# First copies of the down weights' sums: from GpSimd's DMA queue to fixed slots of SP's weight queue

## The chip, the cores and the metric

One core of a Trainium2 chip. The metric is the device time of one execution in microseconds (us), lower is better; the median of several runs is given, and one execution was taken with the hardware profiler. Engines: PE (TensorE, matmuls; PEld its weight loads), ACT (ScalarE), DVE (VectorE), POOL (GpSimd), SP (SyncE, which here only issues DMAs). 16 DMA engines serve all queues of the core; the DMAs that SP issues run on queue q1 and those that POOL issues on q0.

## The reference, cut to what matters

Two decoder layers on 256 tokens of width 2048 in float32: block attention in the first, sliding-window attention with 4 key/value heads in the second, each followed by a convolved, gated feed-forward network with a hidden width of 5504, and a layer norm behind each part:

```python
def conv_ffn(x, w_up, conv_w, conv_b, w_down):
    h = x @ w_up                      # 2048 -> 2 * 5504
    hc = causal_depthwise_conv(h, width 3) + conv_b
    g, v = jnp.split(hc, 2, axis=-1)
    return (jax.nn.gelu(g) * v) @ w_down   # 5504 -> 2048
```

All weights are used once, so each passes through on-chip memory once per run: 770 half-megabyte pieces and a bit.

## The kernel before, in words

**Precision.** Each float32 operand is split into a high part (rounded to the PE's fast format) and a low part, and a product is computed as high x high, high x low and low x high. For weights ACT makes the high part (`high_upto`, L124) and DVE the low part by subtraction (`low_piece`, L133).

**The weight stream.** Weights come from DRAM in "halves" of 128 x 1024 floats (512 KB). A list `source` fixes their order for the whole run. `load_weights` (L98 to L108) issues the next half's DMA on SP (L105) into one of four `raw` buffers; `split_upto` splits a half and then issues the load that takes over its raw buffer; four pairs of buffers hold split halves, besides spare homes in tiles that are idle around a stage's end. `take()` hands the next half to the matmuls and first splits up to three halves ahead. So SP, which executes its instructions in program order, waits in each load until a raw buffer is free, and is paced by PE.

**Slots.** One half's matmuls make a `step()`, which counts the slot up. `at(n, f)` puts a piece of work into the program n slots on; it is written there, in program order, on whichever engine executes it. An engine that waits for none of the stage's data is free to execute it much earlier than PE reaches that slot.

**Up phase.** `FeedForward.run` computes the up-projection in 86 units of two halves (172 slots per layer). The first four units are the "opening" (`ws_opening`, L310 and L322): it uses the first 128 tokens' half of the normalized input first, so that it may start while the second is still being normalized. The other units are `ws_unit`: 8 matmuls with high weights (L292), 8 with low ones (L295) per half. ACT and DVE do the convolution, gate and split of the hidden values beside that.

**Sums for the down phase.** The down-projection computes some products in groups ("quads"), where pairs of hidden blocks and pairs of output column chunks are multiplied with sums of weights and sums of activations, which takes fewer matmuls. There are 16 quads in layer 0 and 18 in layer 1. The sums of weights are formed in DRAM by the DMA engines alone, in a tensor `t` of two halves per quad, by `sum_weights` (L249): steps 0 and 1 copy two blocks into each of t[0] and t[1] (L260, plain copies of 512 KB from DRAM to DRAM); step 2 adds a third block to both parts of t[0] (L262, 512 KB); step 3 adds t[0]'s first part to both parts of t[1] (L264, 512 KB); step 4 adds the fourth block to one part of t[1] (L266, 256 KB). The adding steps are accumulating DMAs issued by POOL; in this kernel the copies are issued by POOL too. `plan_sums` (L268) places the five steps of quad j at slots n0 + j * step + (0, 2, 5, step + 1, step + 4) of the up phase, with n0 = 2 and step = (4 * 43 - 20) // (quads + 3), which is 8 in layer 0 and 7 in layer 1. The down phase loads the sums through the weight stream like any other half (`raw<-t`).

**Around the up phase.** Ahead of it lies the attention's output projection (`project_out`, L345 to L347) with the layer norm: `evac` and `moments` (L438, L443, L565) gather the statistics on DVE, `norm` (L576, L577) applies them, `turn` (L586) transposes on PE. In its last column chunk `late` and `reach` split halves further ahead than usual, into spare homes, so that the opening's eight halves are there. The feed-forward stage's first DMA on POOL is the load of the convolution's weights (L829); in layer 0 four copies of the second layer's bias bands (L276) follow it, and then the sums.

Of the kernel before, what the change touches and what calls it, by code (L numbers as in the profile page):

```python
# [25 lines left out]
FT = DFF // P  # L26
# [23 lines left out]
QUADS = ((10, 6), (10, 8))  # L50
# [23 lines left out]
def trunk(ctx: ExitStack, tc: tile.TileContext, wst, wq, xT_in, x_in, relb, onehot, umask, sinks, conv_in, ln_g, ln_b, out):  # L74
    nc = tc.nc
# [59 lines left out]
    def split_upto(i, behind=None):  # L135
        while todo["low"] <= min(i, n_halves - 1):
            s = todo["low"]
            high_upto(s, behind)
            if len(pieces(s)) == 1:
                low_piece(s, slice(0, HW))  # L140
            placed.pop(s)
            raws.pop(s)
            load_weights()
            todo["low"] += 1
# [4 lines left out]
    def at(n, f, *a, first=False):  # L149

        fs = before.setdefault(slot["now"] + n, [])
        fs.insert(0 if first else len(fs), (f, a))
# [5 lines left out]
    def run(agenda):  # L158
        for n in sorted(n for n in agenda if n <= slot["now"]):
            for f, a in agenda.pop(n):  # L160
                f(*a)  # L161

    def step():
        run(behind)
        slot["now"] += 1
# [3 lines left out]
    def take(ahead=AHEAD):  # L169
        i = nexth["i"]  # L170
        nexth["i"] += 1
        if i in reach:
            run(before)
        split_upto(max(i + ahead, reach.get(i, 0)))
        run(before)
        return halves.pop(i)
# [72 lines left out]
    def sum_weights(q, i):  # L249


        j, t = QUAD_LIST.index(q), tsum[q]
        block = lambda a, b: wq[j][:, a:a + b, :]
        half = lambda k: t[k].rearrange("p (a b) -> p a b", b=512)

        def twice(a):
            return bass.AP(tensor=a.tensor, offset=a.offset, ap=[a.ap[0], [0, 2], [1, 512]])

        if i < 2:
            nc.gpsimd.dma_start(half(i), block(i, 2))  # L260
        if i == 2:
            nc.gpsimd.dma_start(half(0), twice(block(3, 1)), accum_op=ALU.add)  # L262
        if i == 3:
            nc.gpsimd.dma_start(half(1), twice(t[0][:, 0:512]), accum_op=ALU.add)  # L264
        if i == 4:
            nc.gpsimd.dma_start(t[1][:, 512:], wq[j][:, 1, :], accum_op=ALU.add)  # L266

    def plan_sums(l, n0, step):  # L268

        for j, q in enumerate(q for q in QUAD_LIST if q[0] == l):  # L270
            for i, m in enumerate((0, 2, 5, step + 1, step + 4)):
                at(n0 + j * step + m, sum_weights, q, i)
# [25 lines left out]
    def ws_opening(accs, between, done):  # L298

        n0 = nexth["i"]
        nexth["i"] += 2 * len(accs)
        run(before)
        pair = [[halves.pop(n0 + 2 * u + i) for i in range(2)] for u in range(len(accs))]

        def high(u, t, ks):
            part = lambda a: a.rearrange("p (s t c) -> p s t c", s=2, t=2)[:, :, t, :]
            for k in ks:
                nc.tensor.matmul(part(accs[u]), cols(pair[u][k // 8][0], k % 8), part(xT[:, k, :]),  # L310
                                 start=(t == 0 and k == 0), stop=False)

        for u in range(len(accs)):
            between(u)
            high(u, 0, range(KB))
        for c in range(KB // 4):
            between(len(accs) + c)
            for u in range(len(accs)):
                high(u, 1, range(4 * c, 4 * c + 4))
        for u, acc in enumerate(accs):  # L320
            for k in range(KB):
                nc.tensor.matmul(acc[:, 0:T], cols(pair[u][k // 8][1], k % 8), xT[:, k, 0:T],  # L322
                                 start=False, stop=(k == KB - 1))
            step()
            step()
            done(u)
            run(before)

    class Moving:
# [5 lines left out]
        def block(self, ahead=AHEAD):  # L335
            if self.pos % 2 == 0:
                self.half = take(ahead)
            j = self.pos % 2
            self.pos += 1
            return [w[:, j * 512:(j + 1) * 512] for w in self.half]  # L340
# [42 lines left out]
    def acc_tile():  # L383
        return psum.tile([P, 512], F32, name="acc")
# [4 lines left out]
    def four_sums(f0, f1, out):  # L389

        x = ((f0[:, 0:P], f1[:, 0:P]), (f0[:, P:T], f1[:, P:T]))
        s = lambda i: out[:, (i - 1) * P:i * P]
        minus(s(1), x[1][0], x[1][1])
        minus(s(2), s(1), x[0][0])
        minus(s(3), x[0][0], x[1][0])
        nc.vector.tensor_tensor(out=s(4), in0=x[0][1], in1=s(2), op=ALU.add)
# [419 lines left out]
    class FeedForward:  # L816
# [29 lines left out]
        def run(self, rest):  # L846
            l, pool = self.l, self.pool
            norm, (turn, low) = rest
            n0 = nexth["i"]
            cc = COLS[1]  # L850
            for c in cc[:3]:
                norm(c)

            def between(i):
                if i == OPENING - 1:
                    low(cc[0], turn(cc[0]))
                    norm(cc[3])
                if OPENING <= i < OPENING + 3:
                    c = cc[i - OPENING + 1]
                    low(c, turn(c))  # L860
                    if i > OPENING:
                        split_upto(n0 + i + 1)

            def conv(i, s, acc, c):
                w = self.cw[:, i, s, :]
                h = self.place(0)
                nc.scalar.activation(h, acc[:, T:2 * T], AF.Copy)  # L867
                nc.vector.tensor_tensor(out=h, in0=acc[:, 0:T], in1=h, op=ALU.add)  # L868
                nc.vector.tensor_scalar(c, h, w[:, 2:3], w[:, 3:4], op0=ALU.mult, op1=ALU.add)  # L869
                nc.vector.scalar_tensor_tensor(c[:, 1:T], h[:, 0:T - 1], w[:, 1:2], c[:, 1:T], op0=ALU.mult, op1=ALU.add)  # L870
                nc.vector.scalar_tensor_tensor(c[:, 2:T], h[:, 0:T - 2], w[:, 0:1], c[:, 2:T], op0=ALU.mult, op1=ALU.add)  # L871

            def gate(i, g, v):
                nc.vector.tensor_tensor(out=g, in0=g, in1=v, op=ALU.mult)

            def store(i, g):
                b = self.block(i)
                nc.scalar.activation(b[:, 0:T], g, AF.Copy)
                nc.vector.tensor_tensor(out=b[:, T:2 * T], in0=g, in1=b[:, 0:T].bitcast(F32), op=ALU.subtract)

            cs, gs, early = {}, {}, []

            def sums(p):
                if not early:
                    early.append(gbp.tile([P, 2 * D], F32, name="gb"))
                four_sums(gs.pop(2 * p), gs.pop(2 * p + 1), early[0][:, p * 512:(p + 1) * 512])

            def after(u, acc):
                i, s = divmod(u, 2)
                cs[s] = self.place(1 + s)  # L890
                at(0, conv, i, s, acc, cs[s])
                if s == 0:
                    at(1, nc.scalar.activation, cs[0], cs[0], AF.Gelu_apprx_tanh)
                else:
                    at(0, gate, i, cs[0], cs[1])
                    at(1, store, i, cs[0])
                    if i < 2 * S_EARLY:
                        gs[i] = cs[0]
                        if i % 2:
                            at(1, sums, i // 2)  # L900

            plan_sums(l, 2, (4 * FT - 20) // (sum(QUADS[l]) + 3))
            accs = [acc_tile() for _ in range(OPENING)]

            def opened(u):
                after(u, accs[u])
                if u < 2:
                    split_upto(n0 + 2 * OPENING + 2 * u + 1)

            ws_opening(accs, between, opened)  # L910
            for u in range(OPENING, 2 * FT):
                acc = acc_tile()
                ws_unit(acc)
                after(u, acc)
            homes = None
            if l == 0:
                x, h = ([(tile, j) for j in range(n)] for tile, n in ((xT, SPARE), (st, 4)))
                homes = lambda: (x + HALF_BUFS * [None], h + [(self.up, j) for j in range(2)])
            return project_out(self.block, FT, 2 * l + 1, homes, AF.Exp,
                               paired=self.work.rearrange("p a b -> p (a b)"), early_sums=early[0])  # L920
# [123 lines left out]
```

## Time and profile before

| | |
|---|---|
| median of 3 runs | 2104.02 us (2103.35 to 2106.24) |
| profiled execution | 2101.43 us, span of its instructions 2099.7 us |
| PE busy | 98% of the span |
| DVE, ACT, POOL busy | 74%, 50%, 7% |
| bytes moved by DMA | 512.07 MB, of them 416.71 on q1 and 93.24 on q0 |
| mean granted clock of PE | 0.991 |

How to read it: "busy" counts an engine's instructions without its waits; DMA-issuing instructions are not busy time on SP. In the row of 40 slices each digit is the busy share of 52.5 us in tenths. A row of the busy time by stretches has, behind the stretch, its length, then PE, PEld, DVE, ACT and POOL busy with the number of instructions, the granted PE clock, the mean busy share of the 16 DMA engines, and GB/s. The chain of waits is followed back from the last instruction: start, length, what it was waiting for or executing. A row of a queue in the DMA view gives packets, MB, and the time of its packets as a share of 16 engines over the stretch; a row of issues gives the tensors, count, size, and the median time from issue to landing. In a row of the order of time the bracket is the idle time before the instruction and what ended it.

### The profile page before, as it was taken

What the parts mean: (1) busy time and instruction counts of PE and PEld (TensorE: products, weight loads), DVE (VectorE), ACT (ScalarE), POOL (GpSimd) and SP (SyncE); (2) the same over time, 40 slices, a digit from 0 to 9 for tenths busy, and PEclk for the clock granted to TensorE, in tenths of its full rate; (3) what the DMA queues carried; (4) which work ended last, traced back from release to release, by engine and by line L of the source; (5) the groups of instructions that cost most, each with busy time, mean ns of one, the idle gap of its engine ahead of it and who ended that gap; (6) DMA issues with size and microseconds to landing.
All of it is one profiled execution on the core that took longest, in us unless ns stands there. A gap on an engine that the chain in (4) does not pass through costs nothing.

```text
span 2099.7 us, 29222 instructions
## 1 busy us (share of the span) xinstructions
PE 2058.1 (98%) x10974; PEld 1776.7 (85%) x10974; DVE 1547.2 (74%) x2292; ACT 1049.0 (50%) x1467; POOL 151.4 (7%) x196
## 2 busy tenths in 40 slices
PE   9999999799999999999999999889999999999997
PEld 8888888698888888888888888778888888888886
DVE  5655555688888787787776676578888788787767
ACT  5444443345544555465563554435454454455553
POOL 0000001212111000000000000111111100000000
PEclk9999999899999999999999999989999999999999
DMA  8665549999999555578885546989999965558884
GB/s 317 208 221 199 175 167 307 239 280 299 299 296 286 191 189 183 191 264 305 287 284 206 172 145 201 314 223 284 300 303 283 293 212 188 189 203 289 301 295 165
DMA packets 156718, 512.07 MB, mean 244 GB/s; under 512 B 17648, under 2 KB 22320, under 8 KB 155296
## 3 DMA queue, kind: packets, MB, share of 16 engines
q1 hardware_dynamic: 119072, 416.71, 56.3%
q0 software_dynamic: 37216, 93.24, 20.0%
q8 instruction: 86, 1.41, 0.3%
q14 instruction: 56, 0.46, 0.1%
q10 hardware_dynamic: 288, 0.26, 0.0%
HBM read 507.97 MB, written 86.56 MB: 283 GB/s over the span
## 4 chain that ended last, share of the span: by engine, by line
PE 89%; DMA 7%; DVE 2%; ACT 1%; issue 0%; ACTq 0%; POOL 0%; DVEq 0%; POOLq 0%
PE acc L292 38%; PE acc L295 20%; DMA raw<-in_wst_dram 6%; PE acc L546 4%; PE acc L545 4%; PE acc L547 4%; PE acc L345 3%; PE acc L347 3%; PE acc L346 3%; PE acc L310 1%; PE at L546 1%; PE at L547 1%; PE at L545 1%; DMA raw<-t 1%; DVE wl L133 1%; PE acc L322 1%
## 5 line engine op out<-in xcount | busy, mean ns | idle before, releaser
L133 DVE TENSOR_TENSOR wl<-raw,wh 128x1024 fp32r<-128x1024 f32 (+1 forms) x716 | 870.7, 1218 | 447.0 <-ACT wh L124 438.6
L124 ACT ACTIVATE wh<-raw 128x1024 fp32r<-128x1024 f32 (+1 forms) x716 | 755.4, 1056 | 709.1 <-DMA raw<-in_wst_dram 218.3
L292 PE MATMUL acc<-xT,wh 128*128 128x512 f32 x3456 | 872.7, 394 | 0.0
L292 PEld LDWEIGHTS acc<-xT,wh 128*128 128x128 f32 x3456 | 623.4, 189 | 112.9
L295 PEld LDWEIGHTS acc<-xT,wl 128*128 128x128 f32 x3456 | 471.4, 190 | 33.9
L295 PE MATMUL acc<-xT,wl 128*128 128x256 f32 x3456 | 481.8, 282 | 0.0
L545 PE MATMUL acc<-wh,up 128*128 128x512 f32 x336 | 130.8, 389 | 0.0
L546 PE MATMUL acc<-wl,up 128*128 128x512 f32 x336 | 130.8, 389 | 0.0
L547 PE MATMUL acc<-wh,up 128*128 128x512 f32 x336 | 130.7, 389 | 0.0
L870 DVE SCALAR_TENSOR_TENSOR work<-work,cw 128x255 f32<-128x255 f32 x172 | 83.2, 484 | 6.1
L871 DVE SCALAR_TENSOR_TENSOR work<-work,cw 128x254 f32<-128x254 f32 x172 | 83.1, 483 | 6.2
L260 POOL DMA_DIRECT2D t<-in_wq_dram x68 | 76.1, 1119 | 0.0
L869 DVE TENSOR_SCALAR work<-work,cw 128x256 f32<-128x256 f32 x172 | 71.1, 413 | 6.2
L547 PEld LDWEIGHTS acc<-wh,up 128*128 128x128 f32 x336 | 63.1, 188 | 13.2
L545 PEld LDWEIGHTS acc<-wh,up 128*128 128x128 f32 x336 | 63.1, 188 | 13.1
L546 PEld LDWEIGHTS acc<-wl,up 128*128 128x128 f32 x336 | 63.1, 188 | 13.0
L868 DVE TENSOR_TENSOR work<-acc,work 128x256 f32<-128x256 f32 x172 | 71.7, 417 | 1.5 <-ACT work L867 1.5
L161 ACT ACTIVATE work<-work 128x256 f32<-128x256 f32 x86 | 35.9, 418 | 61.6 <-DVE work L871 61.5
L867 ACT ACTIVATE work<-acc 128x256 f32<-128x256 f32 x172 | 62.7, 365 | 6.5 <-PE acc L322 6.5
L264 POOL DMA_DIRECT2D t<-t x34 | 35.6, 1046 | 345.1 <-issue 174.7
L133 DVE TENSOR_TENSOR up<-raw,up 128x1024 fp32r<-128x1024 f32 x30 | 36.5, 1221 | 29.6 <-ACT up L124 29.5
L345 PE MATMUL acc<-wh,xT 128*128 128x512 f32 x144 | 57.8, 401 | 0.0
(209 smaller groups left out, 2227.4 us busy)
## 6 DMA issues: line engine op xcount, KB each, us to landing
raw<-in_wst_dram SPq DMA_DIRECT2D x704, 512.0 KB, 4.6
t<-in_wq_dram POOLq DMA_DIRECT2D x102, 512.0 KB, 11.7
raw<-t SPq DMA_DIRECT2D x68, 512.0 KB, 4.5
t<-t POOLq DMA_DIRECT2D x34, 512.0 KB, 8.3
t<-in_wq_dram POOLq DMA_DIRECT2D x34, 256.0 KB, 7.3
gb<-in_ln_g_dram POOLq DMA_DIRECT2D x4, 1024.0 KB, 8.6
gb<-in_ln_b_dram POOLq DMA_DIRECT2D x4, 1024.0 KB, 11.7
band<-ud SPq DMA_DIRECT2D x4, 512.0 KB
```

The costliest lines, as they stand in the source:

```text
L124: nc.scalar.activation(wh[:, c], raws[s][:, c], AF.Copy)
L133: nc.vector.tensor_tensor(out=wl[:, c], in0=raws[s][:, c], in1=wh[:, c].bitcast(F32), op=ALU.subtract)
L260: nc.gpsimd.dma_start(half(i), block(i, 2))
L292: nc.tensor.matmul(acc, cols(wh, j), xT[:, k, :], start=(k == 0), stop=False)
L295: nc.tensor.matmul(o, cols(wl, j), xT[:, k, 0:T], start=False, stop=(k == KB - 1))
L345: nc.tensor.matmul(acc, sh, wh, start=(k == 0), stop=False)
L545: nc.tensor.matmul(bank(key), a[0], wh[:, c], start=key not in begun, stop=False)
L546: nc.tensor.matmul(bank(key), a[0], wl[:, c], start=False, stop=False)
L547: nc.tensor.matmul(bank(key), a[1], wh[:, c], start=False, stop=stop)
L868: nc.vector.tensor_tensor(out=h, in0=acc[:, 0:T], in1=h, op=ALU.add)
L870: nc.vector.scalar_tensor_tensor(c[:, 1:T], h[:, 0:T - 1], w[:, 1:2], c[:, 1:T], op0=ALU.mult, op1=ALU.add)
L871: nc.vector.scalar_tensor_tensor(c[:, 2:T], h[:, 0:T - 2], w[:, 0:1], c[:, 2:T], op0=ALU.mult, op1=ALU.add)
```

## The change

Steps 0 and 1 of each quad's sum, the plain copies into `t`, are issued by SP instead of POOL, at their slots of the up phase, so in SP's program order they stand between weight loads. The accumulating steps stay on POOL; the first of them now waits for copies that were issued on another engine. The plan begins at slot 12 instead of 2, and the distance between quads becomes (4 * 43 - 30) // (quads + 3): 7 slots instead of 8 in layer 0, 6 instead of 7 in layer 1. Neither copy carries a wait in SP's program. All other lines are as before; line numbers behind `plan_sums` are higher by one.

```diff
@@ sum_weights
         if i < 2:
-            nc.gpsimd.dma_start(half(i), block(i, 2))
+            nc.sync.dma_start(half(i), block(i, 2))
         if i == 2:
             nc.gpsimd.dma_start(half(0), twice(block(3, 1)), accum_op=ALU.add)
@@ plan_sums
         for j, q in enumerate(q for q in QUAD_LIST if q[0] == l):
             for i, m in enumerate((0, 2, 5, step + 1, step + 4)):
                 at(n0 + j * step + m, sum_weights, q, i)
@@ FeedForward.run
-            plan_sums(l, 2, (4 * FT - 20) // (sum(QUADS[l]) + 3))
+            plan_sums(l, 12, (4 * FT - 30) // (sum(QUADS[l]) + 3))
```

## The prediction

> **What bounds the kernel now.** I read the page first, the engines' shares and the 40 slices; then busy time by stretches, the chain of waits, POOL's order of time, and the DMA view of single stretches.
>
> ```profile
> PE 2058.1 (98%) x10974; PEld 1776.7 (85%) x10974; DVE 1547.2 (74%) x2292; ACT 1049.0 (50%) x1467; POOL 151.4 (7%) x196
> ```
>
> ```profile
> POOL 0000001212111000000000000111111100000000
> ...
> DMA  8665549999999555578885546989999965558884
> ```
>
> PE is busy 98%, so at most 41.6 us (2099.7 less 2058.1) can be won from its idle time. POOL works in two stretches, slices 6 to 12 and 25 to 31, one per layer, and there the DMA row stands at 9: POOL does nothing else there than issue the sums' transfers. So the sums are not spread over the up phase; they run as one burst. The busy time by stretches puts the idle PE at the head of each burst:
>
> ```profile
> 360.00:380.00 20.00, 18.90 (x82) 14.89 (x82) 9.62 (x8) 7.81 (x8) 4.00 (x5) 1.00 1.03 320
> 380.00:400.00 20.00, 6.04 (x23) 4.75 (x22) 14.92 (x20) 7.25 (x9) 3.69 (x5) 0.63 0.99 284
> ```
>
> ```profile
> 1340.00:1360.00 20.00, 18.72 (x82) 14.82 (x81) 8.55 (x7) 7.20 (x7) 4.10 (x6) 1.00 1.02 297
> 1360.00:1380.00 20.00, 8.05 (x30) 6.32 (x29) 15.88 (x22) 7.38 (x10) 1.58 (x2) 0.66 0.94 267
> ```
>
> The second number is PE busy of 20 us: idle 1.10 + 13.96 = 15.1 us in layer 0, 1.28 + 11.95 = 13.2 us in layer 1; the DMA share (last but one) is about 1. This is the end of the attention projection, with the layer norm and the opening of the up phase behind it. The chain of waits there:
>
> ```profile
> 318.17 8.78 DMA raw<-in_wst_dram
> ...
> 381.95 8.78 DMA raw<-in_wst_dram
> ...
> 396.82 1.11 PE at L586 x4
> 397.94 0.43 PE acc L345
> ...
> 402.57 0.24 PE acc L345
> ```
>
> From 318 to 391 it goes from one weight load to the next through the raw buffers. The norm's first statistics stand on DVE behind a split that waits for the last of these loads, and PE's transposes (L586) behind the norm. After the wait PE runs at half speed (0.43 us a matmul) until 402.57. POOL's order of time says why the loads are slow then:
>
> ```profile
> 314.16 4.30 POOL L276 DMA_DIRECT2D band<-ud  x4
> 318.45 1.09 POOL L260 DMA_DIRECT2D t<-in_wq_dram  x2
> ```
>
> Nothing ties a sum to a slot of the up phase: POOL starts them right behind the band copies, some 80 us before the opening's matmuls.
>
> **The change, part by part.** *Where the sums start.* The two first copies of each quad stand in SP's program order between weight loads, the first at slot 12; each weight load waits for a raw buffer, so SP gets there only as PE consumes. POOL's first accumulating step (L262) waits for the copy. Slots 0 to 7 are the opening's, and the first unit behind it starts at 431.71:
>
> ```profile
> 431.71 1.84 PE acc L292 x8
> ```
>
> Four halves later, at about 440 us, the first copy goes out, and from 318 until then no sum is in flight (likewise in layer 1, until about 1420). Without sums, in the last down phase, loads come faster:
>
> ```profile
> raw<-in_wst_dram SPq DMA_DIRECT2D x57, 512.0 KB, 4.6
> raw<-t SPq DMA_DIRECT2D x28, 512.0 KB, 4.7
> ```
>
> That is 85 halves in the stretch 1900 to 2060, 1.88 us each, against four per 10.6 us (381.95 less 318.17 over six turns), 2.66 us each, now. The 24 loads of those six turns would take 45 us instead of 64, more than the idle time. Gain: 15.1 + 13.2 us of idle PE, and the half speed behind it (396.82 to 402.57, half of 5.75 is 2.9 us, taken for both layers): 34 us. The four band copies stay where they are at 314 us, so I take **33 us**, bounds 27 and 34. What is late next is the norm itself (393.15 to 396.82 now); its first part lies beside the second half's matmuls already.
>
> *What PE needs in the up phase.* A half's 8 + 8 matmuls take 2.79 us, by the chain:
>
> ```profile
> 1801.46 1.84 PE acc L292 x8
> 1803.30 0.95 PE acc L295 x8
> ```
>
> *What a sum costs the 16 DMA engines.* The DMA view of two stretches in which PE is never idle, 440 to 660 and 1430 to 1680 us:
>
> ```profile
> q0 software_dynamic: 9700, 23.47, 50.3%
> q1 hardware_dynamic: 11343, 41.31, 49.7%
> ```
>
> ```profile
> q1 hardware_dynamic: 13199, 48.07, 50.7%
> q0 software_dynamic: 10708, 25.67, 49.8%
> ```
>
> The shares add to 100%: the engines are full. A half is 0.524 MB, a quad's five transfers 2.36 MB. Weights: 0.497 x 220 us for 78.8 halves, 1.39 us each; 0.507 x 250 for 91.7, 1.38. Sums: 0.503 x 220 for 9.95 quads, 11.1 us each; 0.498 x 250 for 10.9, 11.4. I take 1.38 and 11.25. In these stretches POOL takes what PE leaves, about 22 us a quad, and nobody waits for it.
>
> *The new pace.* A quad now comes every 7 slots in layer 0 and every 6 in layer 1: 19.5 and 16.8 us of PE. The engines need 7 x 1.38 + 11.25 = 20.9 us and 6 x 1.38 + 11.25 = 19.5 us. The copies stand ahead of weights in one queue, so the pace is no longer POOL's to choose: PE is short by 1.4 us for each of 16 quads (22 us) and by 2.7 for each of 18 (49 us). The loads' lead pays for the first of it: a load is issued about 7 halves ahead of its use (four raw buffers and three split halves, 19.5 us), and a turn of landing and split takes 10.6 us at full engines; I take the difference, **9 us** per layer, off, bounds 0 and 14 (a landing of 4.6 with nothing behind it). Loss: 13 + 40 = **53 us**.
>
> By the Trainium skill, DMA: Bandwidth & Descriptors (Issuing engines are not separate DMA queues), DMAs from any issuer run on the same 16 engines, so a move from POOL to SP saves no transfer time. The two shares that add to 1.00 agree.
>
> *The unknown: a DRAM-to-DRAM copy on SP's queue.* From below: what is left of a quad when its accumulating steps are taken out. At the end of the first burst these run without copies; the software queue's share of 653.7 to 666 (L262 with L266), 666 to 674 (L264) and 673.8 to 690 (L266):
>
> ```profile
> q0 software_dynamic: 423, 0.80, 46.5%
> ```
>
> ```profile
> q0 software_dynamic: 272, 0.52, 45.7%
> ```
>
> ```profile
> q0 software_dynamic: 144, 0.26, 10.9%
> ```
>
> 5.72, 3.66 and 1.77 us, so L262, L264 and L266 cost 3.95 + 3.66 + 1.77 = 9.4 us and a copy (11.25 - 9.4)/2 = 0.9 us. From above: SP's own copy in DRAM, of 1 KB rows, in the stretch 60 to 100 us.
>
> ```profile
> q1 hardware_dynamic: 2948, 8.00, 59.1%
> ...
> raw<-in_wst_dram SPq DMA_DIRECT2D x13, 512.0 KB, 3.3
> band<-ud SPq DMA_DIRECT2D x1, 512.0 KB
> ```
>
> 0.591 x 40 = 23.6 us, less 13 loads of 1.38, leaves 5.7 us for the other 1.2 MB, most of it the copy and its load back, 2.5 us for each 0.52 MB. A free copy is the lower end, since SP's copies might hide in gaps. I take 0.9 (inside the 11.25): the copy's rows are those of POOL's. The Trainium skill, same page (Anatomy of one DMA), fits a transfer at 2.0 us plus bytes over 436 GB/s, so 1.2 us of moving for a copy; no run here shows that on SP's queue, and as an estimate the sum would grow by 34 x 2 x 0.3 = 20 us.
>
> *The added wait.* Behind L262 on POOL stand only later steps and the next gb loads, which wait for PE anyway. Do the sums come in time?
>
> ```profile
> 653.71 1.37 POOL L262 DMA_DIRECT2D t<-in_wq_dram  x1
> 666.18 1.03 POOL L264 DMA_DIRECT2D t<-t  x1 [11.10 <-DMA t<-in_wq_dram]
> 673.75 0.83 POOL L266 DMA_DIRECT2D t<-in_wq_dram  x1 [6.54 <-DMA t<-t]
> ```
>
> A quad's steps without copies take 20.0 us, so from 440 us sixteen (at 20.9) end by about 800, from 1420 eighteen by about 1810. The first sums are loaded later than that even now:
>
> ```profile
> 883.53 0.33 SPq L105 DMA_DIRECT2D raw<-t  x1
> ```
>
> ```profile
> 1859.43 0.33 SPq L105 DMA_DIRECT2D raw<-t  x1
> ```
>
> No charge. SP gets 68 issues more, of 0.33 us as these, in 800 us of up phases, and carries no wait for a copy: nothing.
>
> **Sum.** The profiled execution took 2101.4 us (span 2099.7). 2101.4 - 33 + 53 = 2121.4. The runs' median, 2104.0, lies 2.6 higher, so **2124 us**, slower by 20 us.
>
> **Rivals.** *(a) Faster: the transfers keep up.* The place is the 16 engines in the up phase, the price that of a quad, q. The two losses are 16 x (9.66 + q - 19.5) and 18 x (8.28 + q - 16.8), less 18 for the lead: 53 at 11.25, and 33, the gain, at **q = 10.6**, from which down the change wins. If copies on SP's queue hide in gaps, q is 9.4 to 10.3: layer 0 loses nothing, layer 1 18 x 0.9 - 9 = 7 to 18 x 1.8 - 9 = 23 us, and the time is 2078 to 2094. For it: the new pace needs 6.03 MB in 19.5 us and 5.50 MB in 16.8, 309 and 327 GB/s, and 315 (last number) were moved over 20 us with both queues full:
>
> ```profile
> 1300.00:1320.00 20.00, 20.00 (x90) 16.57 (x89) 10.50 (x10) 7.75 (x8) 4.04 (x5) 1.00 1.04 315
> ```
>
> Against it: over the long stretches 23.47 + 41.31 MB in 220 us are 294 GB/s at full share, and accumulating steps, dearer by the byte than loads (3.66 us against 1.38 for 0.52 MB), get a larger part of the mix.
>
> *(b) Slower by much: copies cost more in SP's queue.* At a load's 1.38 us q is 9.4 + 2.8 = 12.2 and the loss 85: 2156 us. At the 2.5 us of the band copy q is 14.4, the loss 161 and the time about 2230. For it: the loads behind a copy wait their turn in one queue, where before they shared by turns. Against it: 4 KB rows instead of 1 KB.
>
> *(c) The opening isn't relieved.* If the norm or the band copies at 314 us set the opening and not the sums, the gain is 5 us at most and the time 2152. Against it: layer 1 has no band copies there and shows nearly the same idle time (13.2 us).
>
> **How the numbers follow.** Forecast 0.46, (a) 0.31, (b) 0.15, (c) 0.08. The forecast's own range, with q from 10.9 to 11.8, the lead and the gain at their bounds, is 2103 to 2145. To hold 8 in 10 the range takes in (c), most of (a) and the cheaper half of (b): **2080 to 2165**. A measurement of this kernel tells about 0.2%, 4 us, from no change, 2100 to 2108. Faster: nearly all of (a), 0.28. Within: the rest of (a) and the forecast's lower edge, 0.09. Slower: most of the forecast, (b) and (c), 0.63.
>
> **What would show it.** Right on the gain: no idle PE over 2 us between 360 and 400 and between 1340 and 1380, no half-speed matmuls at L345 there, raw loads in those windows landing under 5 us, the first L260 at about 440 us of the span. Right on the loss: in the two up phases PE's matmuls of L292 wait for splits (L133, L124) and these for raw loads, in many waits of about a microsecond; DMA share at 1.0 from the first copy to the last; the distance of one quad's first copy to the next about 20.9 and 19.5 us, not 19.5 and 16.8. Wrong: PE without gaps in the up phases (then (a)), or loads landing far over 8 us and quads 23 us apart (then (b)). A weight load of the down phase that waits for L266 would be a wait that I have costed at nothing.

## The result, and the profile after

The changed kernel takes 2070.61 us (median of 4 runs, 2068.69 to 2070.72) against 2105.13 us beside it: ratio 0.9835, 95% interval 0.9817 to 0.9852, faster by 34.5 us. The forecast was slower by 20 us, and the time lies below its range. The profiled execution took 2070.59 us with a span of 2068.7 us, 31.0 us less than before.

The lines that answer to those of before: first the page of the changed kernel.

```profile
PE 2052.5 (99%) x10974; PEld 1773.3 (86%) x10974; DVE 1549.3 (75%) x2292; ACT 1043.0 (50%) x1467; POOL 114.4 (6%) x128
...
POOL 0000000001111110000000000001111111100000
...
DMA  8666548479999998588885545739999999978884
```

PE's idle time fell from 41.6 us to 2068.7 - 2052.5 = 16.2 us. The first copy goes out at 429.7 us in layer 0 and at 1392.8 us in layer 1, 111 and 101 us later than before, and the DMA row dips ahead of each burst. Busy time by stretches, ahead of the up phases and in them (columns as before: PE is the second number, the DMA share the last but one):

```profile
360.00:380.00 20.00, 20.00 (x90) 16.58 (x89) 16.07 (x20) 9.27 (x11) 0.00 (x0) 1.00 0.81 259
380.00:400.00 20.00, 20.00 (x145) 18.57 (x144) 15.15 (x24) 7.84 (x12) 0.00 (x0) 1.00 0.00 1
...
1320.00:1340.00 20.00, 20.00 (x90) 16.56 (x89) 13.29 (x14) 9.19 (x10) 0.00 (x0) 1.00 0.78 262
1340.00:1360.00 20.00, 20.00 (x132) 18.05 (x131) 16.52 (x28) 6.96 (x11) 0.00 (x0) 1.00 0.01 2
```

```profile
440.00:660.00 220.00, 220.00 (x1263) 193.78 (x1262) 181.97 (x305) 107.01 (x157) 26.43 (x27) 1.00 1.00 296
...
1400.00:1600.00 200.00, 200.00 (x1149) 176.20 (x1148) 166.72 (x280) 95.25 (x142) 23.38 (x24) 1.00 1.01 300
```

The idle 15.1 and 13.2 us are gone, and with them the half-speed matmuls (granted clock 1.00, where it was 0.63 and 0.66). Between 380 and 400 us the DMA engines even stand still (share 0.00): the raw buffers are full, and SP's next load waits 26.3 us until a split frees one. And in the up phases, where the loss was forecast, PE is not idle in the stretches shown (nor, in this execution, anywhere from 430 to 910 and from 1400 to 1890 us), though the 16 engines are as full as before. The DMA view of 450 to 740 us says how both hold:

```profile
q1 hardware_dynamic: 19230, 70.05, 64.5%
q0 software_dynamic: 8528, 16.26, 35.6%
...
raw<-in_wst_dram SPq DMA_DIRECT2D x104, 512.0 KB, 7.3
t<-in_wq_dram SPq DMA_DIRECT2D x30, 512.0 KB, 8.2
t<-in_wq_dram POOLq DMA_DIRECT2D x12, 512.0 KB, 12.6
t<-t POOLq DMA_DIRECT2D x12, 512.0 KB, 9.8
```

SP's queue moved 70.05 MB, 133.6 transfers of 0.524 MB, in 0.645 x 290 = 187 us: 1.40 us each, loads and copies taken together. Nine of them in a quad's 19.5 us are 12.6 us, 65%, and that is the share it has. The accumulating steps have the rest. They have not kept the slots' pace. POOL's order of time: the first accumulating step, the first and the fifteenth L266 of layer 0, and the last L266 of layer 1:

```profile
435.29 1.13 POOL L262 DMA_DIRECT2D t<-in_wq_dram  x1 [116.70 <-DMA t<-in_wq_dram]
...
456.72 0.84 POOL L266 DMA_DIRECT2D t<-in_wq_dram  x1 [7.34 <-DMA t<-t]
...
782.92 0.83 POOL L266 DMA_DIRECT2D t<-in_wq_dram  x1 [7.98 <-DMA t<-t]
```

```profile
1817.15 0.83 POOL L266 DMA_DIRECT2D t<-in_wq_dram  x1 [6.90 <-DMA t<-t]
```

Fourteen distances from the first to the fifteenth quad: (782.92 - 456.72)/14 = 23.3 us a quad, where the copies come every 19.5 us (16.8 in layer 1). The use of the tensor `t`, by line:

```profile
L260 SPq DMA_DIRECT2D t<-in_wq_dram x68: 496/497/1336, 429.7 to 1681.8; - x68
L105 SPq DMA_DIRECT2D raw<-t x68: 326/327/327, 865.1 to 2007.8; - x68
```

The last copy of all goes out at 1681.8 us, and the last accumulating step 135 us behind it, at 1817.15. Nobody waits for it: no load of `t` waits for a sum, since the layer's last sums are loaded only late in the down phase. The steps fell behind, and that was free.

### The profile page after: what moved, and what is told of

Its sections match the earlier page's. It is cut to its first block, busy times and chain, and to the rows that moved or that the text cites. A ratio compares the mean times of both kernels' runs of the same rounds, so it can differ in the third digit from the quotient of the medians.

```text
span 2068.7 us, 29221 instructions
## 1 busy us (share of the span) xinstructions
PE 2052.5 (99%) x10974; PEld 1773.3 (86%) x10974; DVE 1549.3 (75%) x2292; ACT 1043.0 (50%) x1467; POOL 114.4 (6%) x128
## 4 chain that ended last, share of the span: by engine, by line
PE 91%; DMA 5%; DVE 2%; ACT 1%; issue 0%; ACTq 0%; POOL 0%; DVEq 0%; POOLq 0%
PE acc L293 38%; PE acc L296 20%; PE acc L346 5%; PE acc L347 5%; PE acc L348 5%; DMA raw<-in_wst_dram 4%; PE acc L547 3%; PE acc L548 3%; PE acc L546 3%; PE acc L311 1%; DVE wl L133 1%; PE at L547 1%; PE at L548 1%; PE at L546 1%; ACT wh L124 1%; DMA raw<-t 1%
## 5 line engine op out<-in xcount | busy, mean ns | idle before, releaser
L293 PE MATMUL acc<-xT,wh 128*128 128x512 f32 x3456 | 873.1, 395 | 0.0
L293 PEld LDWEIGHTS acc<-xT,wh 128*128 128x128 f32 x3456 | 624.1, 189 | 112.5 <-ACT vt L782 0.3
L262 POOL DMA_DIRECT2D t<-in_wq_dram x34 | 45.2, 1329 | 238.0 <-DMA t<-in_wq_dram 237.7
L346 PE MATMUL acc<-wh,xT 128*128 128x512 f32 x144 | 57.9, 402 | 0.0
L264 POOL DMA_DIRECT2D t<-t x34 | 35.1, 1032 | 396.3 <-DMA t<-in_wq_dram 335.9
L348 PE MATMUL acc<-wh,xT 128*128 128x512 f32 x144 | 56.2, 391 | 0.0
## 6 DMA issues: line engine op xcount, KB each, us to landing
t<-in_wq_dram POOLq DMA_DIRECT2D x34, 512.0 KB, 12.6
gb<-in_ln_b_dram POOLq DMA_DIRECT2D x4, 1024.0 KB, 11.8
```

Of the source, the lines that this page charges most:

```text
L293: nc.tensor.matmul(acc, cols(wh, j), xT[:, k, :], start=(k == 0), stop=False)
L346: nc.tensor.matmul(acc, sh, wh, start=(k == 0), stop=False)
L348: nc.tensor.matmul(acc, sl, wh, start=False, stop=(k == self.nk - 1))
```

## The experiments

**Theory A**: the gain is the later start alone (no sum in flight while the opening's weights are loaded); in the up phase only what SP's queue carries, weights and copies, must keep the slots' pace, and the accumulating steps take what is left. **Theory B**: SP's queue itself makes the copies cheaper. **Theory C**: the engines are elastic and carry what is asked. The rule of the prediction: a quad's whole transfer price falls due within its slots. Of the diff's two edits, the slot numbers alone change nothing: with the copies on POOL the order of instructions on POOL and on SP is the same for slots 2 and 8 apart as for 12 and 7 apart, since only these two engines issue the sums and each has its own order. This is read from the program and was not run. So the other experiments start from the changed kernel.

**Only the first quad's copies on SP's queue.**

```diff
-            nc.sync.dma_start(half(i), block(i, 2))
+            (nc.sync if q[1:] == (0, 0) else nc.gpsimd).dma_start(half(i), block(i, 2))
```

> The changed kernel, but only the first quad's two copies of each layer go through SP's queue; all other copies are issued by POOL again, behind the first quad's first accumulating step, so the burst starts at slot 12 and then runs at POOL's own pace. Theory A (the gain is the later start alone; which queue carries the copies after that costs and brings nothing): 2071 us, within 4 us of the changed kernel, PE without gaps. Theory B (SP's queue itself makes copies cheaper, the gain needs all copies on it): clearly slower than the changed kernel, 2080 us or more.

Measured: 2066.21 us (2065.36 to 2067.99), ratio 0.9826 (0.9810 to 0.9843). Four copies of 68 suffice; the time is 4.4 us under the changed kernel's, 0.4 us outside what Theory A allowed, on the fast side. DMA view of 440 to 660 us and busy time by stretches:

```profile
q1 hardware_dynamic: 11519, 41.94, 49.9%
q0 software_dynamic: 9626, 23.35, 49.3%
```

```profile
300.00:400.00 100.00, 100.00 (x492) 84.45 (x491) 70.44 (x86) 46.56 (x56) 4.85 (x5) 1.00 0.61 209
...
440.00:660.00 220.00, 220.00 (x1263) 193.60 (x1262) 183.29 (x308) 109.74 (x159) 40.22 (x50) 1.00 0.99 298
```

The queues are back at the halves of the kernel before, the burst runs at POOL's own pace, and the idle time ahead of the up phase is gone all the same. Theory B falls: the queue did not bring the gain, the wait did that ties POOL's first accumulating step to a copy in SP's program order.

**The same copies, some 28 loads earlier.** The plan is called when the feed-forward stage is set up instead of in the up phase.

```diff
+            plan_sums(self.l, 6, (7, 6)[self.l])
...
-            plan_sums(l, 12, (4 * FT - 30) // (sum(QUADS[l]) + 3))
```

> The changed kernel with the same copies on the same queue, but the plan begins some 28 loads earlier, inside the attention's output projection, ahead of the up phase. Theory A (the loads of the opening were held up by the sums being in flight there): the idle PE ahead of the up phase comes back in part or in full, 15 to 34 us, 2085 to 2105 us. Theory B (the queue brought the gain): 2071 us.

Measured: 2084.67 us (2 runs, 2083.0 to 2086.34), ratio 0.9913 (0.9887 to 0.9939), 14 us over the changed kernel's 2070.61: the idle time comes back in part, and the time lies a hair under the range given. Busy time by stretches:

```profile
380.00:400.00 20.00, 11.87 (x51) 9.56 (x50) 15.98 (x24) 7.61 (x11) 2.69 (x3) 0.74 0.82 225
...
1340.00:1360.00 20.00, 16.19 (x70) 13.12 (x69) 15.51 (x22) 6.92 (x9) 1.03 (x1) 0.91 0.96 281
```

The idle PE is back where it was, 8.1 and 3.8 us of it, with the lower clock behind it. It is less than before, probably since the first copy waits until 342.7 us here and not 318.5; that was not tried apart. What counts is which transfers are in flight ahead of the opening, whatever queue they use.

**Quads 4 slots apart.**

```diff
-            plan_sums(l, 12, (4 * FT - 30) // (sum(QUADS[l]) + 3))
+            plan_sums(l, 12, 4)
```

> The changed kernel with the quads 4 slots apart instead of 7 and 6. Theory A (only weights and copies must keep the slots' pace: 4 + 2 transfers of 1.4 us, 8.4 us in the 11.2 us of 4 slots; the accumulating steps fall behind and take what is left, ending before they are needed): no loss, 2071 us within 4 us, the accumulating steps over 24 us a quad while the copies run. The predicted rule (a quad's whole transfer price falls due within its slots): short by 4 x 1.38 + 11.25 - 11.2 = 5.6 us for each of 34 quads less the lead, some 170 us, 2240 us.

Measured: 2073.85 us (2071.96 to 2075.66), ratio 0.9864 (0.9845 to 0.9884): 3.2 us over the changed kernel and 7.6 over the version with four copies, run beside it, not the 170 us of the predicted rule. DMA view of 440 to 560 us, busy time, and the first and last L266 of layer 0:

```profile
q1 hardware_dynamic: 9122, 33.20, 72.1%
q0 software_dynamic: 3565, 6.81, 32.1%
```

```profile
440.00:620.00 180.00, 178.15 (x1022) 156.66 (x1021) 144.38 (x244) 82.62 (x123) 21.58 (x22) 1.00 1.03 325
```

```profile
456.26 0.84 POOL L266 DMA_DIRECT2D t<-in_wq_dram  x1 [9.64 <-DMA t<-t]
...
796.52 0.83 POOL L266 DMA_DIRECT2D t<-in_wq_dram  x1 [6.99 <-DMA t<-t]
```

Six transfers in 11.2 us are 75% by Theory A, and SP's queue has 72.1%. The copies are out long before the accumulating steps, which end about where they ended in the changed kernel: (796.52 - 456.26)/15 = 22.7 us a quad. PE loses 1.85 us in these 180, and 4.0 us in the whole run in waits of L293 for splits: a small loss.

**Quads 2 slots apart.** The place where Theory A itself must lose.

```diff
-            for i, m in enumerate((0, 2, 5, step + 1, step + 4)):
+            for i, m in enumerate((0, 1, 5, 6, 7)):
...
-            plan_sums(l, 12, (4 * FT - 30) // (sum(QUADS[l]) + 3))
+            plan_sums(l, 12, 2)
```

> The changed kernel with the quads 2 slots apart (the five steps at slots 0, 1, 5, 6, 7 of a quad). Theory A: now weights and copies alone need 2 + 2 transfers of 1.4 us, 5.6 us, in the 5.6 us of 2 slots, with nothing left for the accumulating steps, which still take about a third of the engines: 5.6 / 0.67 = 8.4 us, short by 2.8 us for 34 quads, 95 us less 9 us of lead per layer, some 75 us, 2145 us; at least 20 us over the changed kernel. The predicted rule (a quad's whole price): 2 x 1.38 + 11.25 - 5.6 = 8.4 us for 34 quads, some 270 us, 2340 us. Elastic transfers: 2071 us.

Measured: 2141.83 us (2 runs, 2141.14 to 2142.51), ratio 1.0184 (1.0163 to 1.0204): 71 us over the changed kernel, where Theory A had worked out 75, the predicted rule 270 and elastic transfers nothing. Busy time, the DMA view of 440 to 560 us, and who waited for whom:

```profile
440.00:570.00 130.00, 106.13 (x552) 89.88 (x551) 75.84 (x129) 43.65 (x64) 14.65 (x15) 0.95 1.01 302
...
1440.00:1580.00 140.00, 115.03 (x576) 97.87 (x575) 80.19 (x136) 46.73 (x69) 15.63 (x16) 0.90 1.01 306
```

```profile
q1 hardware_dynamic: 8474, 30.83, 71.5%
q0 software_dynamic: 3131, 5.99, 30.7%
```

```profile
PE acc L293 <- ACT wh L124: 48.7, 28, 4.8
```

PE is idle 23.9 and 25.0 us, 48.8 together, nearly all in waits for splits, and the clock falls to 0.95 and 0.90. This is how the forecast loss would have looked in the changed kernel; here SP's queue alone asks for the whole of the engines and gets 71.5%. Theory C falls with it.

**Two tensors of sums in turn**, so that a copy waits for the accumulating steps of the quad two before.

```diff
-    tsum = {q: dram.tile([2, P, HW], F32, name=f"t{i}") for i, q in enumerate(QUAD_LIST)}
+    ring = [dram.tile([2, P, HW], F32, name=f"t{i}") for i in range(2)]
+    tsum = {q: ring[i % 2] for i, q in enumerate(QUAD_LIST)}
```

> The changed kernel, but all quads share two tensors of sums in turn, so a copy on SP waits until the accumulating steps of the quad two before are done, and the weights behind it wait too: the accumulating steps may no longer fall behind by more than two quads. The sums that the down phase loads are those of the last quads, so its products are not the reference's; the amount of work is the same. Theory A (the forecast loss failed to come because the accumulating steps may fall behind): the loss comes back, a quad needs 20 to 24 us where its slots give 19.5 and 16.8: 40 to 130 us more than the changed kernel, 2110 to 2200 us. Theory C (the transfers are elastic and keep up with the slots when they must): 2071 us.

Measured: 2179.34 us (2 runs, 2178.99 to 2179.7), ratio 1.0363 (1.0337 to 1.0389): 109 us over the changed kernel. SP's waits and busy time (lines are one higher here):

```profile
SPq L261 <- DMA t<-in_wq_dram: 177.6, 26, 7.6
SPq L261 <- DMA t<-t: 166.3, 26, 10.3
```

```profile
440.00:880.00 440.00, 417.01 (x2352) 362.95 (x2351) 335.25 (x545) 198.94 (x295) 46.04 (x47) 1.00 0.90 261
...
1440.00:1960.00 520.00, 466.55 (x2482) 403.72 (x2481) 357.74 (x569) 216.12 (x314) 50.63 (x52) 0.94 0.81 237
```

SP stands 344 us in front of copies, the weights behind them, and PE is idle 23.0 + 53.5 us. So a loss does come once the accumulating steps may not fall behind. But it comes by another mechanism than the forecast's. The stretches above reach beyond the last sum; the queues' shares while the sums run, at 460 to 800 and at 1500 to 1800 us, are

```profile
q1 hardware_dynamic: 19781, 72.00, 59.5%
q0 software_dynamic: 10200, 19.45, 35.5%
...
q1 hardware_dynamic: 14853, 54.09, 52.1%
q0 software_dynamic: 8790, 16.74, 33.1%
```

The engines are at 95% and 85%, not full, and yet POOL's steps take 23.2 us a quad in layer 0, from the first to the last, (803.47 - 454.92)/15, and 23.1 in layer 1, (1837.37 - 1445.21)/17. So here it is the chain of dependent transfers, one behind the other, that sets the time. The changed kernel's 23.3 us a quad may be set by the same chain rather than by the engines; the two were not tried apart there.

**Copies on SP's queue, slots of before.**

```diff
-            plan_sums(l, 12, (4 * FT - 30) // (sum(QUADS[l]) + 3))
+            plan_sums(l, 2, (4 * FT - 20) // (sum(QUADS[l]) + 3))
```

> The changed kernel with the slots of before: the plan begins at slot 2, quads 8 and 7 slots apart; copies on SP's queue. Theory A (what counts is that the start is tied to the up phase by SP's program order, not the slot numbers): 2071 us within 4 us. If the opening needs the engines for itself until slot 12: 2075 to 2085 us.

Measured: 2067.48 us (2065.71 to 2069.23), ratio 0.9828 (0.9811 to 0.9845). This is within the 4 us that Theory A allowed. Slot 2 is late enough; the slot numbers of the diff bring nothing that these runs can tell.

**The changed kernel and the first experiment once more, on one chip.**

> The changed kernel itself once more, on the same chip as the three runs beside it. All theories: 2068 to 2072 us.

> Only the first quad's two copies of each layer on SP's queue, all others on POOL, once more, beside the changed kernel on one chip. If the queue is of no account: the changed kernel's time within 2 us. If copies in the weights' queue cost PE anything in the up or down phase (3 us of idle time stood in the changed kernel's first down phase): 2 to 5 us faster than the changed kernel, 2065 to 2068 us.

Measured: 2070.53 us (2067.26 to 2074.56), ratio 0.9845 (0.9826 to 0.9865), and 2067.45 us (2065.12 to 2068.57), ratio 0.9828 (0.9814 to 0.9843). The medians differ by 3.1 us (4.4 the first time), in the range given for copies that cost PE something, but the intervals overlap. The profiled executions show where such a difference can lie, the first down phase, for the changed kernel, its repetition, the first experiment and the run with the slots of before:

```profile
880.00:1130.00 250.00, 247.05 (x1109) 203.50 (x1108) 185.44 (x196) 137.63 (x141) 5.21 (x8) 1.00 0.78 261
```

```profile
880.00:1130.00 250.00, 247.68 (x1108) 204.10 (x1107) 188.26 (x198) 139.05 (x142) 5.21 (x8) 1.00 0.76 259
```

```profile
880.00:1130.00 250.00, 250.00 (x1127) 207.06 (x1126) 189.78 (x199) 139.60 (x143) 5.21 (x8) 1.00 0.76 266
```

```profile
880.00:1130.00 250.00, 249.35 (x1124) 205.92 (x1123) 187.13 (x197) 138.84 (x142) 5.21 (x8) 1.00 0.77 266
```

PE is idle 2.95, 2.32, 0.00 and 0.65 us there, and 0.42 in the first experiment's repetition. But the run with the slots of before has all 68 copies on SP's queue, too, and took 2067.48 us on the same chip, as little as the version with four. So the 3 us are not shown to be the price of copies on SP's queue as such; why the down phase differs stays open. In the repetition PE was idle in the first up phase, too, 3.0 us between 430 and 880 us, in waits of L293 for splits. This is the sign of the loss that the prediction named, at a few us; the profiles of the changed kernel's first run, of the old slots and of both runs with four copies show none of it.

## Why the prediction was wrong, point by point

- **What bounds the kernel now**: right. The idle PE was the sums in flight ahead of the opening; the runs with the start moved away from it (four copies, old slots) and back into it show it.
- **Where the sums start**: right. The first copy went out at 429.7 us (forecast about 440), and POOL's first accumulating step waited 116.7 us for it.
- **The gain, 33 us**: right. The span fell by 31.0 us and the medians by 34.5.
- **The prices**: a half at 1.38 us and a quad at 11.25 hold as totals (1.40 measured; 2 x 1.40 and 0.356 x 290/12.4 = 8.3 us of accumulating steps are 11.1). The split was off: a copy on SP's queue, at one price with the loads, costs 1.40 us, between the bounds of 0.9 and 2.5, and the accumulating steps 8.3 instead of 9.4.
- **The new pace**: this step failed. "The engines need 7 x 1.38 + 11.25 = 20.9 us" put the accumulating steps' 9.4 us into every quad's slots. Only SP's queue is tied to the slots, 9 x 1.40 = 12.6 of 19.5 us and 8 x 1.40 = 11.2 of 16.8. The accumulating steps are issued by POOL, one behind the other, and took 23.3 us a quad instead; they ended 135 us behind the last copy and still in time. The loss was 53 us in the forecast; measured, PE was idle 0.0 us from 430 to 910 and from 1400 to 1890 us in the one profile of the changed kernel and 3.0 us in the other. The sum over a whole up phase would have told that no loss is forced: 172 halves of 1.38 and 16 quads of 11.25 are 417 us of the engines in 480 us of PE. That sum alone is not enough, though: with two tensors in turn the transfers are the same, and 109 us were lost, since there somebody waits for the steps that fall behind.
- **The full share**: I read 100% in the kernel before as need. The burst filled what PE left, as the prediction itself said, so a full share did not tell that a denser plan must cost PE time.
- **The added wait and the time left**: right that nobody waits. That the last step came at 1817 us, where the estimate for layer 1 was about 1810, is partly luck: the sums started 27 us earlier than forecast (1392.8 against 1420) and took 23.3 us a quad, not 19.5 to 20.9. The prediction held a rate near the one that mattered (20.0 us a quad without copies, nobody waiting) and used it only to ask whether the sums come in time.
- **The range**: the forecast's own upper edge was added up too low. With q at 11.8, no lead and a gain of 27 the loss is 90 us and the time 2104 - 27 + 90 = 2167, not 2145. The sign does not hang on it.
- **Rivals**: the result is (a)'s sign and nearly its time, but not its mechanism. A quad still took 11.1 us of the engines, not 9.4 to 10.3, and the transfers did not keep up with the slots; they fell behind unpunished. Copies on SP's queue do not hide either: with quads 2 slots apart they cost 71 us. (b) at its cheaper end had the price of a copy, a load's, but not the loss, for the same reason as the forecast. (c) fell with the idle PE.

## What to carry to other kernels

Before charging a transfer to a stage's pace, ask who waits for it and when. In this kernel only the queue that the bound engine's data stands in had to keep pace, and work in another queue that may fall behind cost nothing, as the sum over the whole stage fits and its end is in time. A DMA share of 100% beside a burst that nobody waits for says nothing of need. To keep background transfers out of a tight spot one ordered wait at the head of the burst is enough; here 4 copies of 68 did what all 68 do.

## What the runs showed of the hardware

- The two queues do not always share the engines half and half: with accumulating transfers alone in POOL's queue and loads and copies in SP's, SP's had 64.5%, 72.1% and 71.5% at full engines (7, 4 and 2 slots), with 2.3, 2.6 and 2.7 packets for one of POOL's. At 7 slots that is all it asked for (65%); at 2 slots it asked for the whole. With most copies on POOL, in the first experiment, the halves were 49.9% and 49.3%. The Trainium skill, DMA: Bandwidth & Descriptors (Queues, rings and completion order), has each engine take packets in turn from the queues that it has work for; the counts do not show one for one where POOL has one or two accumulating transfers in flight at a time. Whether POOL's queue then lacked work at some engines was not tried apart.
- A transfer in DRAM that accumulates 512 KB took 3.7 us of the engines (L264 in the kernel before), against 1.40 us for a plain transfer of that size on SP's queue (loads and copies taken together, changed kernel).
